# A two-layer hybrid transformer on one core: w_out, w_o and the merge gates multiplied in 1024-column panels

## The chip, the core and the metric

The kernel runs on one NeuronCore of a Trainium2 chip, in fp32 throughout. The metric is the device time of one execution in microseconds (us), as a median over runs; lower is better. Engines are named as in the profile: PE is the matrix engine (TensorE) and PEld its weight loads, DVE is VectorE, ACT is ScalarE, POOL is GpSimd, SP only issues transfers here. The program is written with a tile framework: tiles come from pools with a fixed number of buffers, and a scheduler fixes, before the program ever runs, the order in which each engine's instructions stand. On the chip each engine takes its own list in that order and waits at an instruction until what it needs is there.

## The reference

256 tokens of width 2048 pass through two layers and a last norm. Cut to what matters here:

```python
# layer 1
h = rmsnorm(x, g_mix) @ w_in                      # split into z, xBC, dt, q, k, v, qi, ki, wi
y_ssd = ssd(...) * silu(z), normed                # [256, 1024]
y_att = attention over the top keys               # [256, 1024]
x = x + concat(y_ssd, y_att) @ w_out              # w_out [2048, 2048]
x = x + square(relu(rmsnorm(x, g_mlp) @ w_up)) @ w_down
# layer 2
h = rms_norm(x, ln1_w) @ w_in_2                   # 10792 columns; the last 4096 are two merge gates
o_a = nsa_attention(...)                          # compressed, selected and window branch, [256, 1024]
o_b = gated_delta_rule(...)                       # [256, 1024]
m = sigmoid(gate_a) * (o_a @ w_pa) + sigmoid(gate_b) * (o_b @ w_pb)
x = x + m @ w_o                                   # w_o [2048, 2048]
x = x + square(relu(rms_norm(x, ln2_w) @ w_up_2)) @ w_down_2
out = rms_norm(x, ln_f_w)
```

## The kernel before

**One product is three matmuls.** Every fp32 operand is split into a high part rounded to fp32r and a low part, the rest. A product of a 128 x 128 block of activations (the left side, held as `xh`, `xl`) with a 128 x 512 block of weights (`wa`, `wb`) is xh wa + xh wb + xl wa, three matmuls of 512 columns that add up in one PSUM bank. Weights stream in from HBM once, 1 MB at a time, into a ring of three tiles `wst`; ACT rounds each 128 x 1024 half into `whi`, DVE subtracts it into `wlo`. There are four buffers of `whi` and four of `wlo`.

**Two ways to multiply a matrix.** `panel` makes 512 columns: for each of 16 k-tiles and both token halves one product, so 96 matmuls, into two PSUM banks, one of the tag `mm0` and one of `mm1`. `wide` makes 1024 columns for 256 tokens and takes the k-tiles in eight pairs. Six pairs are plain (eight products each). Two pairs, `SPAIRS = (2, 5)`, are multiplied as 2 x 2 blocks by seven products in place of eight (the Winograd form of Strassen's method): the weight sums `t13` and `t24` are made by DVE, the sums of the left side come from `forms`, made once (`a_forms`). `wide` needs eight accumulators at once: P2, P3, P4 and E from its first product on, P1, P5, P6 and P7 from the first seven-product pair on. `shared` adds them up to the four outputs.

**PSUM has eight banks,** in four tags of two: `mm0`, `mm1`, `tp` (transposes) and `sx` (small products of the attentions and scans). `panel` uses the first two tags alone. `wide` uses all four; it takes P2, P3, P4 and E from `mm0` and `mm1` when a counter `turn` is even and from `tp` and `sx` when it is odd, the other four accumulators from the other two tags, and adds 1 to `turn`. A tile of a tag can only be written once the tile before the last one of this tag has been read for the last time.

**Where it is used before.** `wide` makes w_up and w_down of both layers (15 calls in each layer; the last of w_down is `panel` twice). `panel` makes everything else: w_in, w_out (in four panels, the k-tiles of the attention half first), the merge gates (L1298), w_pb and w_pa (L1301), w_o (L1327).

**The order around the places that change.** In layer 1 the tail of the SSD scan (lines L715 to L754, products in `sx`, then L772, L777 and the transposes of `xsd` in `tp` by `x_to_act`, L345) is written just ahead of w_out. In layer 2 the attention (from L1078 to L1290: transposes in `tp`, scores and outputs in `sx`) is written just ahead of the merge: first o_b with `gate_b` and w_pb, then o_a with `gate_a` and w_pa. A group of the attention is two heads: scores against two kinds of keys (L1256), softmax for two token halves and two kinds (L606 add, L611 max, L616 exp, L618 to L621, L622 scaling), transposes of the probabilities (L1266, L1271, copied out by L1268 and L1273; the compressed branch's L1279, copied by L1281), and the outputs (L1286 to L1290). There are four such groups. The transposes of O (L876) and the small products that make the compressed keys come ahead of them.

Of the kernel before, what the change touches and what calls it, by code (L numbers as in the profile page):

```python
# [57 lines left out]
def build(ctx, tc, I, out, tap=None, upto=99):  # L58
# [176 lines left out]
    def wide(w, r0, c0, lhs, forms):  # L235
# [8 lines left out]
        ns = len(SPAIRS)  # L244
# [20 lines left out]
        for j in range(8):  # L265
# [3 lines left out]
            if j not in SPAIRS:  # L269
# [96 lines left out]
    def flat(ap):  # L366
        return ap.rearrange("p k c -> p (k c)")

    def ffn(X, act, forms, w_up, w_down, r, after, tail=0):
        for s_ in range(4):  # L370
# [27 lines left out]
            for P in range(2):  # L398
# [8 lines left out]
                out_ = shared(B)  # L407
                for i, l, part, bank in out_:
                    x = X[2 * P + 1 - l][:, i]
                    V.tensor_tensor(x, part, x, op=OP.add)  # L410
                for i, l, part, bank in out_:
                    x = X[2 * P + 1 - l][:, i]
                    V.tensor_tensor(x, bank, x, op=OP.add)
# [401 lines left out]
    ffn(X, xn, xforms, I["w_up"][0], I["w_down"][0], r, after1)  # L815
# [478 lines left out]
    M = []  # L1294
    for which, (o_, w_, mc) in enumerate(((ob, "w_pb_2", 2048), (oa, "w_pa_2", 0))):
        for p in range(4):
            ps = panel(w_in2, 0, 16, 6696 + mc + p * 512, 512, at_k(xn))
# [28 lines left out]
    for p in range(4):  # L1326
        ps = panel(I["w_o_2"][0], 0, 16, p * 512, 512, at_k(M))  # L1327
        for t in range(2):
            V.scalar_tensor_tensor(X[p][:, t], ps[t], 0.5, X[p][:, t], op0=OP.mult, op1=OP.add)
        q = quarter("xn")  # L1330
        x_to_act(X[p], q, g_ln2[:, 4 * p:4 * p + 4], xforms, p)
        xn.append(q)
        for t in range(2):
            sumsq(ssx[:, t, p:p + 1], X[p][:, t])
# [52 lines left out]
```

## Time and profile before

| | |
|---|---|
| median of 3 runs | 2650.08 us (2646.22 to 2652.0) |
| the profiled execution, its own time | 2654.01 us |
| its span, first to last instruction | 2652.2 us |
| PE busy | 2623.1 us, 99% |
| DVE, ACT busy | 1917.3 us (72%), 1411.5 us (53%) |
| mean granted TensorE clock | 0.997 of full |

Busy is the time in which an engine has at least one instruction under way. A matmul is shown for longer than it holds the next one back, since matmuls are pipelined: a 512-column matmul is shown with some 0.39 us, and the next starts 0.23 us later. So the time of a stretch of PE is read from how many matmuls start in it.

### The profile page before, as it was taken

The numbers are of one execution on the slowest core, as the hardware profiler recorded it, in microseconds if no ns is written. First come the engines' busy times: TensorE is split into PE (matmuls) and PEld (weight loads), VectorE is DVE, ScalarE is ACT, GpSimd is POOL, SyncE is SP. The second block draws the span as 40 slices with busy tenths as digits, with TensorE's granted clock in tenths as the row PEclk, the third lists the DMA queues.
The fourth block names the chain that finished last, engine by engine and source line by source line (L and its number), as shares of the span: only waits on it lengthen the run. The fifth ranks groups of instructions, "written<-read, shape, count | busy, mean of one in ns | idle before, by whom it ended". The sixth has DMA issues, their size and how long they took to land.

```text
span 2652.2 us, 32498 instructions
## 1 busy us (share of the span) xinstructions
PE 2623.1 (99%) x12656; PEld 2195.1 (83%) x12656; DVE 1917.3 (72%) x2593; ACT 1411.5 (53%) x1876; POOL 39.2 (1%) x46
## 2 busy tenths in 40 slices
PE   8999999999999999999999999999999999999998
PEld 8998888888887888888888887888888888888887
DVE  5767767787887887676754767455678888888886
ACT  5465455546556556554533554444456455465564
POOL 0000000000000000000100000000000000000000
PEclk9999999999999999999999999999999999999999
DMA  7454555565555555653432743556555555555544
GB/s 237 144 172 159 175 188 182 175 207 191 190 205 176 191 191 191 213 194 127 131 97 86 252 161 113 181 191 212 193 190 176 207 200 183 203 190 191 206 175 175
DMA packets 192153, 478.63 MB, mean 180 GB/s; under 512 B 9128, under 2 KB 50047, under 8 KB 191999
## 3 DMA queue, kind: packets, MB, share of 16 engines
q1 hardware_dynamic: 185840, 467.57, 52.3%
q10 hardware_dynamic: 6158, 8.99, 1.0%
q8 instruction: 99, 1.62, 0.2%
q14 instruction: 56, 0.45, 0.0%
HBM read 472.32 MB, written 4.21 MB: 180 GB/s over the span
## 4 chain that ended last, share of the span: by engine, by line
PE 92%; DMA 3%; DVE 2%; ACT 2%; issue 1%; ACTq 0%; POOL 0%; POOLq 0%; SPq 0%; DVEq 0%
PE mm L250 21%; PE mm L193 13%; PE mm L194 13%; PE mm L192 13%; PE tp L250 11%; PE sx L250 10%; DMA wst<-in_w_down_dram 2%; DVE wlo L262 2%; PE sx L982 1%; ACT whi L261 1%; PE sx L977 1%; PE tp L345 1%; PE mm L390 1%; DMA wst<-in_w_up_dram 1%; PE tp L876 0%
## 5 line engine op out<-in xcount | busy, mean ns | idle before, releaser
L208 DVE TENSOR_TENSOR wlo<-wst,whi 128x1024 fp32r<-128x1024 f32 (+6 forms) x416 | 475.8, 1147 | 321.6 <-ACT whi L207 320.7
L261 ACT ACTIVATE whi<-wst 128x1024 fp32r<-128x1024 f32 x480 | 476.8, 1005 | 379.3 <-PE mm L250 164.1
L207 ACT ACTIVATE whi<-wst 128x1024 fp32r<-128x1024 f32 (+6 forms) x416 | 414.7, 998 | 467.4 <-PE mm L194 437.2
L262 DVE TENSOR_TENSOR wlo<-wst,whi 128x1024 fp32r<-128x1024 f32 x480 | 543.5, 1155 | 140.7 <-ACT whi L261 133.1
L193 PE MATMUL mm<-wlo,x2h 128*128 128x512 f32 (+3 forms) x736 | 279.4, 380 | 0.8 <-DVE wlo L208 0.8
L194 PE MATMUL mm<-whi,x2l 128*128 128x512 f32 (+3 forms) x736 | 279.3, 380 | 0.0
L192 PE MATMUL mm<-whi,x2h 128*128 128x512 f32 (+3 forms) x736 | 279.1, 380 | 0.0
L261 ACT ACTIVATE whi<-t 128x1024 fp32r<-128x1024 f32 x120 | 127.3, 1061 | 150.5 <-PE mm L250 76.8
L262 DVE TENSOR_TENSOR wlo<-t,whi 128x1024 fp32r<-128x1024 f32 x120 | 146.9, 1224 | 80.1 <-ACT whi L261 79.7
L250 PE MATMUL mm<-whi,xnh 128*128 128x512 f32 x432 | 169.0, 391 | 0.0
L250 PE MATMUL mm<-whi,xnl 128*128 128x512 f32 x432 | 168.4, 390 | 0.0
L250 PE MATMUL mm<-wlo,xnh 128*128 128x512 f32 x432 | 168.2, 389 | 0.0
L193 PEld LDWEIGHTS mm<-wlo,x2h 128*128 128x128 f32 x736 | 139.0, 189 | 21.2 <-DVE wlo L208 1.4
L192 PEld LDWEIGHTS mm<-whi,x2h 128*128 128x128 f32 x736 | 139.0, 189 | 20.2 <-issue 1.1
L194 PEld LDWEIGHTS mm<-whi,x2l 128*128 128x128 f32 x736 | 138.9, 189 | 19.9 <-issue 0.9
L192 PE MATMUL mm<-whi,xnh 128*128 128x512 f32 (+3 forms) x416 | 153.0, 369 | 2.0 <-ACT whi L207 1.6
L193 PE MATMUL mm<-wlo,xnh 128*128 128x512 f32 (+3 forms) x416 | 152.2, 366 | 0.0
L194 PE MATMUL mm<-whi,xnl 128*128 128x512 f32 (+3 forms) x416 | 150.9, 366 | 0.1
L250 PE MATMUL mm<-whi,hTh 128*128 128x512 f32 x378 | 148.4, 393 | 0.0
L250 PE MATMUL mm<-wlo,hTh 128*128 128x512 f32 x378 | 147.7, 391 | 0.0
L250 PE MATMUL mm<-whi,hTl 128*128 128x512 f32 x378 | 147.5, 390 | 0.0
L250 PEld LDWEIGHTS mm<-whi,xnl 128*128 128x128 f32 x432 | 81.1, 188 | 17.0
(532 smaller groups left out, 5303.7 us busy)
## 6 DMA issues: line engine op xcount, KB each, us to landing
wst<-in_w_up_dram SPq DMA_DIRECT2D x128, 1024.0 KB, 4.9
wst<-in_w_down_dram SPq DMA_DIRECT2D x128, 1024.0 KB, 5.5
wst<-in_w_in_dram SPq DMA_DIRECT2D x84, 1024.0 KB, 5.0
wst<-in_w_out_dram SPq DMA_DIRECT2D x16, 1024.0 KB, 5.2
wst<-in_w_o_dram SPq DMA_DIRECT2D x16, 1024.0 KB, 5.0
wst<-in_w_in_dram SPq DMA_DIRECT2D x16, 780.0 KB, 4.4
wst<-in_w_in_dram SPq DMA_DIRECT2D x12, 824.0 KB, 4.5
wst<-in_w_in_dram SPq DMA_DIRECT2D x12, 736.0 KB, 6.3
```

What stands on the lines that cost most here:

```text
L192: PE.matmul(ps[t][:, :n], xh[:, sl], wa, start=kt == first, stop=False)
L193: PE.matmul(ps[t][:, :n], xh[:, sl], wb, start=False, stop=False)
L194: PE.matmul(ps[t][:, :n], xl[:, sl], wa, start=False, stop=kt == last)
L207: S.activation(a[:, :2 * n], src, AF.Copy)
L208: V.tensor_tensor(b[:, :2 * n], src, a[:, :2 * n].bitcast(F32), op=OP.subtract)
L250: PE.matmul(B[b], x, y, start=left[b] == total[b], stop=left[b] == 1)
L261: S.activation(a[:, :n], src, AF.Copy)
L262: V.tensor_tensor(b[:, :n], src, a[:, :n].bitcast(F32), op=OP.subtract)
L345: PE.transpose(ps[:, kk, t, :], x[:, t, (k0 + kk) * 128:(k0 + kk + 1) * 128], ident)
L390: PE.transpose(pv[:, kk, t, :], us[t, l][:, c:c + 128], ident)
L977: PE.matmul(ps[:, i * 64:(i + 1) * 64].rearrange("p (m b) -> p m b", b=b), N[:, i], half(T[:, i], 0), start=True, stop=True)
L982: PE.matmul(ps[:, i * 64:(i + 1) * 64].rearrange("p (m b) -> p m b", b=b), P[:, i], half(Tt[:, i], 1), start=True, stop=True)
```

## The change

w_out and w_o become two calls of `wide` each, and each merge gate becomes two. The sums of the left side, which the feed-forward layers make on the way from the transposes, are made here by a new helper `forms_of` from the two parts (high plus low) of the activations that are there already. `wide` takes the number of its seven-product pairs from `forms` and the order of the pairs as an argument: w_out uses the pairs 5 and 7 in the order 4, 5, 6, 7, 0, 1, 2, 3. The code that adds the four outputs to X moves out of `ffn` into `add_blocks`; `add_wide` replaces `add_panel`. The factor 0.5 of w_o moves into the split of M. Calls of `wide` now stand ahead of the two feed-forward layers, so that `turn` is 0 and 1 at w_out, 17 to 20 at the merge gates, 21 and 22 at w_o.

```diff
+    def forms_of(act, pairs):
+
+        forms = {}
+        for j in pairs:
+            f = s2([128, 2, 2, 128], name="ff")
+            k0 = 2 * (j % 2)
+            h, l = (flat(a[:, k0:k0 + 2]).bitcast(F32) for a in act[j // 2])
+            V.tensor_tensor(f.rearrange("p k t c -> p (k t c)"), h, l, op=OP.add)
+            a_forms(f, forms, j)
+        return forms
+
-    def wide(w, r0, c0, lhs, forms):
+    def wide(w, r0, c0, lhs, forms, order=range(8)):
...
-        ns = len(SPAIRS)
+        ns = len(forms)
...
-        for j in range(8):
+        for j in order:
...
-            if j not in SPAIRS:
+            if j not in forms:
...
+    def add_blocks(B, P):
+        out_ = shared(B)
+        for i, l, part, bank in out_:
+            x = X[2 * P + 1 - l][:, i]
+            V.tensor_tensor(x, part, x, op=OP.add)
+        for i, l, part, bank in out_:
+            x = X[2 * P + 1 - l][:, i]
+            V.tensor_tensor(x, bank, x, op=OP.add)
...
-    def add_panel(ps, p, scale, act, gain, ssx, forms):
-        for t in range(2):
-            V.scalar_tensor_tensor(X[p][:, t], ps[t], scale, X[p][:, t], op0=OP.mult, op1=OP.add)
-        q = quarter("xn")
-        x_to_act(X[p], q, gain[:, 4 * p:4 * p + 4], forms, p)
-        act.append(q)
-        for t in range(2):
-            sumsq(ssx[:, t, p:p + 1], X[p][:, t])
+    def add_wide(w, act, P, xn, gain, ssx, forms, xforms, order=range(8)):
+        B, _ = wide(w, 0, P * 1024, at_k(act), forms, order)
+        add_blocks(B, P)
+        for p in (2 * P, 2 * P + 1):
+            q = quarter("xn")
+            x_to_act(X[p], q, gain[:, 4 * p:4 * p + 4], xforms, p)
+            xn.append(q)
+            for t in range(2):
+                sumsq(ssx[:, t, p:p + 1], X[p][:, t])
...
-    for p in range(4):
-        ps = panel(I["w_out"][0], 0, 16, p * 512, 512, at_k(mix), order=list(range(8, 16)) + list(range(8)))
-        add_panel(ps, p, 1.0, xn, g_mlp, ssx, xforms)
+    forms = forms_of(mix, (5, 7))
+    for P in range(2):
+        add_wide(I["w_out"][0], mix, P, xn, g_mlp, ssx, forms, xforms, (4, 5, 6, 7, 0, 1, 2, 3))
...
     M = []
+    forms = forms_of(xn, SPAIRS)
     for which, (o_, w_, mc) in enumerate(((ob, "w_pb_2", 2048), (oa, "w_pa_2", 0))):
-        for p in range(4):
-            ps = panel(w_in2, 0, 16, 6696 + mc + p * 512, 512, at_k(xn))
-            th = sp([128, 2, 512], name="mth")
-            for t in range(2):
-                S.activation(th[:, t], ps[t], AF.Tanh, scale=rh[:, t:t + 1])
-            ps = panel(I[w_][0], 0, 8, p * 512, 512, at_k(o_))
...
+        for P in range(2):
+            B, _ = wide(w_in2, 0, 6696 + mc + P * 1024, at_k(xn), forms)
+            ths = {}
+            for i, l, part, bank in shared(B):
+                V.tensor_tensor(part, bank, part, op=OP.add)
+                S.activation(part, part, AF.Tanh, scale=rh[:, i:i + 1])
+                ths[2 * P + 1 - l, i] = part
+            for p in (2 * P, 2 * P + 1):
+                ps = panel(I[w_][0], 0, 8, p * 512, 512, at_k(o_))
...
-    for p in range(4):
-        ps = panel(I["w_o_2"][0], 0, 16, p * 512, 512, at_k(M))
-        for t in range(2):
-            V.scalar_tensor_tensor(X[p][:, t], ps[t], 0.5, X[p][:, t], op0=OP.mult, op1=OP.add)
...
+    forms = forms_of(M, SPAIRS)
+    for P in range(2):
+        add_wide(I["w_o_2"][0], M, P, xn, g_ln2, ssx, forms, xforms)
```

The scheduler sets the order anew. Three places of PE's list follow; L1256 and the like are lines of before, and the attention's lines have moved down by 15 in the changed kernel (L1256 is L1271 now); L192 to L194 are the three matmuls of `panel`, L261 (L250 before) those of `wide`.

**PE in the second group of the attention, before.** The scores of a group (into `sx`), and what stands between them and behind them: w_pb's panel (`mm_`; obh and obl are the parts of o_b).

```order
L1256 MATMUL sx<-ksT,nqT 128x128 x2
L192 MATMUL mm_13585<-whi,obh 128x512
L193 MATMUL mm_13585<-wlo,obh 128x512
L194 MATMUL mm_13585<-whi,obl 128x512
L1256 MATMUL sx<-ksT,nqT 128x256 x2
L1256 MATMUL sx<-kwT,nqT 128x128 x2
L192 MATMUL mm_13586<-whi,obh 128x512
L193 MATMUL mm_13586<-wlo,obh 128x512
L1256 MATMUL sx<-kwT,nqT 128x256 x2
L194 MATMUL mm_13586<-whi,obl 128x512
L192 MATMUL mm_13585<-whi,obh 128x512
L193 MATMUL mm_13585<-wlo,obh 128x512
```

The same place in the changed kernel, from the scores to the transposes of both kinds of keys:

```order
L1271 MATMUL sx<-ksT,nqT 128x128 x2
L1271 MATMUL sx<-ksT,nqT 128x256 x2
L1271 MATMUL sx<-kwT,nqT 128x128 x2
L1271 MATMUL sx<-kwT,nqT 128x256 x2
L1281 MATMUL tp<-idt,NP_13235 128x128
L1281 MATMUL tp<-idt,NP_13250 128x128
L1281 MATMUL tp<-idt,NP_13235 128x128
L1281 MATMUL tp<-idt,NP_13250 128x128
L1286 MATMUL tp<-idt,NP_13250 128x128 x2
L1281 MATMUL tp<-idt,NP_13277 128x128
L1281 MATMUL tp<-idt,NP_13292 128x128
L1281 MATMUL tp<-idt,NP_13277 128x128
```

The panel's matmuls that stood between the scores and the transposes are gone from there. No matmul of a panel or of `wide` stands between the first transposes of O and the last four transposes of the fourth group, which follow here, with what comes behind them (`x2h` is the left side of the merge gate):

```order
L1294 MATMUL tp<-idt,Pc_13076 15x128
L1294 MATMUL tp<-idt,Pc_13102 15x128
L1294 MATMUL tp<-idt,Pc_13076 15x128
L1294 MATMUL tp<-idt,Pc_13102 15x128
L261 MATMUL tp<-whi,x2h 128x512
L261 MATMUL tp<-wlo,x2h 128x512
L261 MATMUL tp<-whi,x2l 128x512
L261 MATMUL tp<-whi,x2h 128x512
L1301 MATMUL sx<-NTc,vcm 128x2x128
```

So the merge gate begins behind the last transposes of the attention, with accumulators in `tp` and `sx`; before, 298 matmuls of panels stood in that stretch.

**PE at the end of the SSD scan, before.** The scan's last product (L751) stands fourteen matmuls ahead of the first transposes of `xsd` (L345), which are for the first half of y_ssd; between and behind them stands w_out's first panel on the attention half (`yatt`):

```order
L192 MATMUL mm_2979<-whi,yatth 128x512
L193 MATMUL mm_2979<-wlo,yatth 128x512
L194 MATMUL mm_2979<-whi,yattl 128x512
L192 MATMUL mm_2980<-whi,yatth 128x512
L345 MATMUL tp<-idt,xsd 128x128 x2
L193 MATMUL mm_2980<-wlo,yatth 128x512
L345 MATMUL tp<-idt,xsd 128x128 x6
L194 MATMUL mm_2980<-whi,yattl 128x512
L192 MATMUL mm_2979<-whi,yatth 128x512
```

The same place in the changed kernel (L765 is the scan's last product, L356 the transposes for both halves; `sfh` is a left sum of `forms`):

```order
L761 MATMUL sx<-xdd,Bm 128x512
L754 MATMUL sx<-xdt,E 128x64 x4
L261 MATMUL mm_3004<-whi,yattl 128x512
L765 MATMUL sx<-ST,acc 128x512
L356 MATMUL tp<-idt,xsd 128x128 x16
L261 MATMUL mm_3002<-whi,sfh 128x512
L261 MATMUL mm_3002<-wlo,sfh 128x512
L261 MATMUL sx<-whi,sfh 128x512
```

The first pair of `wide`, 24 matmuls of which the last is shown, lies ahead of the scan's last product. Between that and the sixteen transposes there is no matmul now, and the pair behind them (`sfh`) puts products into `tp`, which the transposes use first.

## Rows read from the trace of the kernel before

**Rows 1.** The page's head: span, then busy time, share and instructions of each engine.

```profile
span 2652.2 us, 32498 instructions
PE 2623.1 (99%) x12656; PEld 2195.1 (83%) x12656; DVE 1917.3 (72%) x2593; ACT 1411.5 (53%) x1876; POOL 39.2 (1%) x46
```

**Rows 2.** Stretches: start:end, length, busy time and instructions by engine, granted clock, DMA.

```profile
core 0: us, PE busy (x) PEld busy (x) DVE busy (x) ACT busy (x) POOL busy (x), PEclk, DMA share, GB/s
1662.00:1860.00 198.00, 198.00 (x888) 163.84 (x886) 101.61 (x97) 86.51 (x90) 0.00 (x0) 1.00 0.59 197
2048.00:2122.00 74.00, 74.00 (x328) 61.33 (x327) 62.39 (x70) 37.52 (x39) 0.00 (x0) 1.00 0.57 201
1560.60:1564.10 3.50, 3.50 (x32) 3.43 (x31) 0.00 (x0) 1.38 (x3) 0.00 (x0) 1.00 0.51 196
1564.10:1570.90 6.80, 6.80 (x23) 5.86 (x23) 2.88 (x20) 1.72 (x5) 0.00 (x0) 0.50 0.00 0
```

**Rows 3.** Stretches for line L193 alone, one panel matmul in three.

```profile
321.50:334.10 12.60, 5.88 (x15) 2.63 (x14) 1.00 0.61 191
1540.30:1569.10 28.80, 8.70 (x21) 4.10 (x21) 0.91 0.42 141
1540.30:1656.10 115.80, 40.47 (x100) 19.00 (x99) 0.97 0.35 117
```

**Rows 4.** Timeline: first transposes of O; first scores of each group on DVE.

```profile
1540.39 1.03 PE L876 MATMUL tp<-idt,O 128*128 128x128 f32 x8
...
1569.15 0.42 DVE L606 TENSOR_TENSOR NP<-sx,Bt 128x256 f32<-128x256 f32 x1 [1.86 <-PE sx L1256]
...
1592.66 0.43 DVE L606 TENSOR_TENSOR NP<-sx,Bt 128x256 f32<-128x256 f32 x1 [2.30 <-PE sx L1256]
...
1615.35 0.42 DVE L606 TENSOR_TENSOR NP<-sx,Bt 128x256 f32<-128x256 f32 x1 [4.93 <-PE sx L1256]
...
1638.66 0.42 DVE L606 TENSOR_TENSOR NP<-sx,Bt 128x256 f32<-128x256 f32 x1 [5.39 <-PE sx L1256]
```

**Rows 5.** Timeline of DVE's softmax: second kind of keys (group 1), first kind's end (2).

```profile
1577.53 0.43 DVE L1273 COPY NT<-tp 128x256 f32<-128x256 f32 x1
...
1579.78 1.22 DVE L208 TENSOR_TENSOR wlo<-wst,whi 128x1024 fp32r<-128x1024 f32 x1
...
1582.99 0.69 DVE L622 TENSOR_TENSOR NP<-NP,su 128x512 f32<-128x512 f32 x1
...
1597.69 0.69 DVE L622 TENSOR_TENSOR NP<-NP,su 128x512 f32<-128x512 f32 x1
...
1599.31 0.42 DVE L1273 COPY NT<-tp 128x256 f32<-128x256 f32 x1 [0.59 <-PE tp L1271]
```

**Rows 6.** Timeline of a group's tail: probabilities out, outputs, next scores.

```profile
1654.95 0.52 PE L1266 MATMUL tp<-idt,NP 128*128 128x128 f32 x3
...
1656.16 0.61 PE L1279 MATMUL tp<-idt,Pc 128*15 128x128 f32 x4
...
1657.63 0.69 PE L1286 MATMUL sx<-NTc,vcm 15*128 15x256 f32 x2
...
1661.34 0.60 PE L1290 MATMUL sx<-NT,KVw 128*128 128x256 f32 x2
...
1638.02 0.61 PE L1256 MATMUL sx<-ksT,nqT 128*128 128x128 f32 x4
```

**Rows 7.** Timeline from the SSD scan's last product to y_ssd's last low parts.

```profile
321.55 1.02 PE L751 MATMUL sx<-ST,acc 128*128 128x512 f32 x2
...
323.28 1.22 DVE L208 TENSOR_TENSOR wlo<-wst,whi 128x1024 fp32r<-128x1024 f32 x1
...
328.71 1.60 POOL L159 TENSOR_TENSOR rg<-rv,mhalf 128x2 f32<-128x2 f32 x1 [3.66 <-DVE rv L157]
...
333.61 1.90 DVE L174 SCALAR_TENSOR_TENSOR yssdl<-tp,P1T,yssdh 128x256 fp32r<-128x256 f32 x4
```

**Rows 8.** Groups by line and shape: count, busy us, mean ns, idle us before and releaser.

```profile
L390 PE MATMUL mm<-idt,cu 128*128 128x128 f32 x64 | 15.6, 285 | 4.5 <-ACT cu L378 4.5
L390 PE MATMUL tp<-idt,cu 128*128 128x128 f32 x32 | 8.9, 291 | 5.3 <-ACT cu L378 5.3
```

More of the change, by code (lines that the diff above doesn't have):

```diff
@@ L367, in flat, with ffn @@
         return ap.rearrange("p k c -> p (k c)")
-    def ffn(X, act, forms, w_up, w_down, r, after, tail=0):
+    def add_blocks(B, P):
[6 more added lines that the diff above has]
+            V.tensor_tensor(x, bank, x, op=OP.add)
+    def ffn(act, forms, w_up, w_down, r, after, tail=0):
         for s_ in range(4):
@@ L406, in ffn @@
                 B, _ = wide(w_down, s_ * 2048, P * 1024, at_k(hT), hforms)
[L407 to L413, printed above, removed]
+                add_blocks(B, P)
                 if s_ == 3:
@@ L783, in build @@
     ssx = tiny([128, 2, 4], "ssx", bufs=2)
[L785 to L792 removed]
+    def add_wide(w, act, P, xn, gain, ssx, forms, xforms, order=range(8)):
+        B, _ = wide(w, 0, P * 1024, at_k(act), forms, order)
+        add_blocks(B, P)
+        for p in (2 * P, 2 * P + 1):
[4 more added lines that the diff above has]
+                sumsq(ssx[:, t, p:p + 1], X[p][:, t])
     X = x_panels()
@@ L813, in after1 @@
             nc.scalar.dma_start(xsave[:, p], X[p])
-    ffn(X, xn, xforms, I["w_up"][0], I["w_down"][0], r, after1)
+    ffn(xn, xforms, I["w_up"][0], I["w_down"][0], r, after1)
     if upto == 2:
@@ L1294, in build @@
     M = []
+    forms = forms_of(xn, SPAIRS)
     for which, (o_, w_, mc) in enumerate(((ob, "w_pb_2", 2048), (oa, "w_pa_2", 0))):
-        for p in range(4):
-            ps = panel(w_in2, 0, 16, 6696 + mc + p * 512, 512, at_k(xn))
-            th = sp([128, 2, 512], name="mth")
-            for t in range(2):
-                S.activation(th[:, t], ps[t], AF.Tanh, scale=rh[:, t:t + 1])
-            ps = panel(I[w_][0], 0, 8, p * 512, 512, at_k(o_))
-            if which == 0:
-                m = sp([128, 2, 512], name="M")
-                M.append(m)
-                for t in range(2):
-                    V.scalar_tensor_tensor(m[:, t], th[:, t], 1.0, ps[t], op0=OP.add, op1=OP.mult)
-            else:
-                for t in range(2):
-                    V.scalar_tensor_tensor(th[:, t], th[:, t], 1.0, ps[t], op0=OP.add, op1=OP.mult)
-                    V.tensor_tensor(M[p][:, t], M[p][:, t], th[:, t], op=OP.add)
+        for P in range(2):
[7 more added lines that the diff above has]
+                ps = panel(I[w_][0], 0, 8, p * 512, 512, at_k(o_))
+                if which == 0:
+                    m = sp([128, 2, 512], name="M")
+                    M.append(m)
+                    for t in range(2):
+                        V.scalar_tensor_tensor(m[:, t], ths[p, t], 1.0, ps[t], op0=OP.add, op1=OP.mult)
+                    continue
+                for t in range(2):
+                    th = ths[p, t]
+                    V.scalar_tensor_tensor(th, th, 1.0, ps[t], op0=OP.add, op1=OP.mult)
+                    V.tensor_tensor(M[p][:, t], M[p][:, t], th, op=OP.add)
                 q = quarter("mT")
@@ L1317, in build @@
                             PE.transpose(pv[:, kk, t], M[p][:, t, (k0 + kk) * 128:(k0 + kk + 1) * 128], ident)
-                    split(pt, flat(q[0][:, k0:k0 + 2]), flat(q[1][:, k0:k0 + 2]))
+                    split(pt, flat(q[0][:, k0:k0 + 2]), flat(q[1][:, k0:k0 + 2]), 0.5)
                 M[p] = q
@@ L1325, in build @@
     ssx = tiny([128, 2, 4], "ssx", bufs=2)
-    for p in range(4):
-        ps = panel(I["w_o_2"][0], 0, 16, p * 512, 512, at_k(M))
-        for t in range(2):
-            V.scalar_tensor_tensor(X[p][:, t], ps[t], 0.5, X[p][:, t], op0=OP.mult, op1=OP.add)
[L1330 to L1334, printed above, removed]
+    forms = forms_of(M, SPAIRS)
+    for P in range(2):
+        add_wide(I["w_o_2"][0], M, P, xn, g_ln2, ssx, forms, xforms)
     r = x_rstd(ssx, "r4")
@@ L1361, in after2 @@
         nc.sync.dma_start(o[:, 1024:1536], X[2][:, t])
-    ffn(X, xn, xforms, I["w_up_2"][0], I["w_down_2"][0], r, after2, tail=8)
+    ffn(xn, xforms, I["w_up_2"][0], I["w_down_2"][0], r, after2, tail=8)
 _INS = ["x", "g_mix", "w_in", "conv_w", "conv_b", "dt_bias", "a_log", "d_skip", "g_ssd", "g_q", "g_k", "g_kidx",
```

## The prediction, made before the changed kernel had run

> **What bounds the kernel now.** I read the page's head first: PE is busy for 2623.1 of 2652.2 us [rows 1], so time goes where PE starts matmuls, and any hole in its list is lost. Then the stretches. In 74 us of `wide` in a feed-forward layer 328 matmuls start, one in 0.2256 us; DVE is busy for 62.4 of these 74 us, 84%, so it keeps up there [rows 2]. In the panels of the merge it is busy for 101.6 of 198 us, 51% [rows 2]. Both ways of multiplying are bound by the number of matmuls. The third view is what PE does while DVE and ACT work through a chain of small steps: in the 115.8 us of the attention one panel line of three has 100 matmuls, two of which began before it, and at the end of the SSD scan one has 15 in 12.6 us [rows 3]. Panels fill PE while it would wait for softmax. The change touches just these panels.
>
> **What the change removes.** A 2048 x 2048 matrix costs four panels of 96 matmuls, 384; two calls of `wide` cost 2 x (6 x 24 + 2 x 21) = 372. Four such matrices (w_out, two gates, w_o) give 48 matmuls fewer, 48 x 0.2256 = **10.8 us** less.
>
> **What it moves, the attention.** `panel` used `mm0` and `mm1` alone, so it could run while the attention held `tp` and `sx`. `wide` needs all four tags, and `turn` is 17 at the first gate, so its first four accumulators are the ones in `tp` and `sx`: it can't start while the attention passes tiles through these. The order shows what the scheduler made of that: no matmul of a weight matrix from the first transposes of O to the last transposes of the fourth group, 298 before; w_pb stands behind the gate and comes no earlier. The 298 are not lost, they run later. What is lost is the cover: PE's time in that stretch is now as long as the chain, T, and before its own work and small waits in it took 115.8 - 298 x 0.2256 = 48.6 us. The loss is T - 48.6.
>
> T by pieces. The head, from the first transposes of O to the first scores on DVE, took 1569.15 - 1540.39 = 28.8 us [rows 4]; 61 panel matmuls (3 x 21 less the two that began before) were in it [rows 3], 13.8 us. If they all delayed it, it takes 15.0 us bare, if none, 28.8; I take the middle, 21.9, since handovers between small instructions make most of it but ACT and DVE also split weights there. A group took 23.5, 22.7 and 23.3 us [rows 4]. Bare, by steps: softmax for the first kind of keys 1592.66 to 1598.38, 5.7 us, in which DVE split no weights [rows 4, 5]; to the copy of the transposes 0.9 [rows 5]; from such a copy to the end of the second softmax 1577.53 to 1583.68, 6.2 us with one split of 1.22 in it [rows 5], of which I keep 5.4; then the tail, which the fourth group shows: its last transposes begin at 1654.95, some 0.15 us after the scaling, and its outputs end at 1661.94 [rows 6], 7.1; scores until DVE has them, 1638.02 to 1638.66, 0.6 [rows 4, 6]. Sum 19.8 us. All of that with PE at full clock. PE hardly works during the softmaxes, and what the clock does then one stretch tells: after 3.5 us in which PE issued only tiny products (32, of 7 to 15 columns for the most part) the granted clock was 0.50 for 6.8 us, that is 1.2 GHz in place of 2.4 [rows 2]. At that level the outputs, 4.3 us from 1657.63 to 1661.94 [rows 6], take some 3.4 more (what is not waiting doubles), and some twenty scores and transposes on the path, 0.11 us each [rows 4, 6], another 2.1. I take the outputs at half and the rest at full clock, 23.2, near 23: **what the panels took away from DVE, the clock takes back**. So T = 21.9 + 3 x 23 + 14.0 (the fourth group without outputs and scores: 5.7 + 0.9 + 5.4 + 2.0) = 104.9, and the loss is **56.3 us**. Bounds: 15.0 + 3 x 19.8 + 14.0 = 88.4, a loss of 39.8; and 28.8 + 3 x 25.3 + 15.3 = 120, a loss of 71.4.
>
> On the clock the Trainium skill (TensorE: Matmul & The Clock Gate, section "What's actually happening") says that the throttled state is the default and activity releases it; the 0.50 of [rows 2] agrees. By that rule all of the bare stretch would run at 1.2 GHz, which is rival 2 below; by the full clock of the rows around it, the group's 19.8 us would stand.
>
> The first matmuls of the gate then start at half clock: 6.8 us at half [rows 2] cost **3.4 us**, bounds 0 and 6.8 (if w_out pays the same).
>
> **What it moves, the SSD scan.** In w_out only pair 4 fits beside the scan (`mm` tags); pair 5 needs `tp`, which y_ssd's transposes use. From the scan's last product to the last low part of y_ssd is 321.5 to 335.5 us [rows 7]; in the 12.6 us to 334.1 stood some 42 panel matmuls (3 x 15, less those at the edges) [rows 3], 9.5 us of cover. The chain behind it, DVE, POOL's power of 1.60 us twice [rows 7], transposes, split, stays; DVE loses about two splits of 1.22 us and gets sums for `forms` in their place, perhaps 1.2 us less. After the transposes 16 products can run before the split of `t24` is there, about 1.9 us short. 9.5 - 1.2 + 1.9, **10 us**, bounds 6 and 13 (half clock behind the hole).
>
> **What it adds.** `forms_of`, `t13` and `t24` for eight calls, additions in `shared`: on DVE, hidden where `wide` runs as in the feed-forward layers, at 84% [rows 2], and at the first gate behind 48 matmuls (10.8 us) of two plain pairs whose weights are split early. Without that cover it would be some 5 us for each matrix (two times add, four small sums, split). At the border between two calls the transposes wait for the last addition, with four to nine matmuls to fill. Such borders in w_up wait 9.8 us in 16 calls [rows 8], 0.6 each; four borders at w_out and w_o, **2.5 us**, bounds 0 and 8 (each near 2). The DMAs stay as many and as large on SP's queue, of 2 k-tiles x 1024 columns in place of 4 x 512; w_up's have that shape already, in the stretch at 0.2256 us [rows 2].
>
> **Sum.** -10.8 + 56.3 + 3.4 + 10 + 2.5 = +61.4. On the profiled execution, 2654.0, that is 2715; the median of the runs shown is 3.9 us lower, so I forecast **2712 us** for the median. With all low ends 2650.1 - 10.8 + 39.8 + 6 = 2685, with all high ends 2650.1 - 10.8 + 71.4 + 6.8 + 13 + 8 = 2739.
>
> **Rivals.**
> 1. The chain hurries: with no weights to split, DVE and ACT answer at once and the clock recovers in every burst. For it: the head's bare bound, and the first softmax without a split, 5.7 us. Against it: the 0.50 row, and 19.8 us for a group is already the sum without splits. T = 88.4, 2652.5 + 39.8 - 56.3 = about 2695 us.
> 2. All of the stretch at half clock: T = 120, 2712 + 15 = 2727 us. For it the 0.50 row; against it that the clock was full again after 6.8 us.
> 3. DVE becomes the bound in w_out and at the gate, where sums of the left side come on top of 84%: 5 us for each of three matrices more, 2727 us. Against it the slack at the panels of w_pb and w_pa between.
> 4. The other side: PE is not held up, because it starts the gate's matmuls past the attention's waiting ones. Then the 48 matmuls count and the rest stays hidden: 2650.1 - 10.8 + 2.5 = 2642 us, faster. It decides from the point where T falls to 48.6 us, or where PE leaves the order of its list. Against it: four groups of two softmaxes are 44 us on DVE and ACT [rows 5], and outputs, scores and head stand in series with them.
> The Trainium skill (TensorE: Matmul & The Clock Gate, "Step-by-step: what each phase is for") says that matmuls stay in program order and only weight loads are pulled ahead, which speaks against rival 4; in the rows shown PE's starts follow its list.
>
> **How the numbers follow.** The forecast as summed 0.56, rival 1 0.17, rival 2 0.14, rival 3 0.09, rival 4 0.04. The range 2688 to 2738 takes in rivals 1 to 3 but for their outer tails, which with rival 4 are 2 in 10. About 0.2%, 5.3 us, is what a measurement of this kernel can tell from no change. Only rival 4 is faster (0.03) or the same (0.01), all others slower, 0.96.
>
> **What would show it.** In the changed profile: about 105 us from the first transposes of O to the fourth group's last, with PE busy for less than half of it and a granted clock near 0.5 in much of it; groups 23 us apart on DVE though it splits no weights; a hole of 8 to 10 us after the scan's last product; elsewhere 0.2256 us a matmul and 48 matmuls fewer. I am wrong if the groups come 17 us apart or less, if matmuls of the gate start among the attention's, or if holes appear inside the `wide` calls that follow.

## The result, and the profile after

The changed kernel takes **2723.77 us** (median of 5 runs, 2719.12 to 2727.02) against 2650.08 (2646.22 to 2652.0): ratio 1.0278, 95% interval 1.0263 to 1.0294. It is 73.7 us slower; forecast were 2712, in a range of 2688 to 2738. Its profiled execution took 2723.77 us as well, 69.8 more than the one of before (2654.01), and the accounts below are made against those 69.8.

The page's head of the changed kernel answers to [rows 1]: PE is busy 19 us longer with 48 matmuls fewer, and the span holds 69.7 us more, so 51 us of it are PE standing still.

```profile
span 2721.9 us, 32676 instructions
...
PE 2642.0 (97%) x12608; PEld 2201.6 (81%) x12608; DVE 2034.0 (75%) x2773; ACT 1446.8 (53%) x1922; POOL 38.9 (1%) x46
```

The windows of the changed kernel (columns as in [rows 2]): first the five pieces of the attention, from the first transposes of O over the first scores of each group on DVE (they answer to [rows 4]) to the first matmul of the gate; then the start of the gate; then w_out behind the scan's last product; last a stretch of `wide` in a feed-forward layer.

```profile
1549.20:1576.20 27.00, 18.19 (x98) 13.92 (x96) 11.04 (x30) 10.29 (x21) 0.00 (x0) 0.67 0.19 71
1576.20:1600.50 24.30, 16.58 (x48) 10.81 (x48) 11.32 (x45) 5.80 (x20) 0.00 (x0) 0.59 0.00 0
1600.50:1624.30 23.80, 15.36 (x48) 9.86 (x48) 10.77 (x32) 5.61 (x20) 0.00 (x0) 0.64 0.00 0
1624.30:1648.20 23.90, 15.37 (x48) 9.86 (x48) 10.85 (x33) 5.71 (x20) 0.00 (x0) 0.64 0.00 1
1648.20:1662.50 14.30, 6.64 (x28) 4.53 (x29) 10.11 (x31) 5.20 (x19) 0.00 (x0) 0.71 0.00 1
...
1549.20:1662.50 113.30, 72.13 (x269) 48.99 (x268) 54.08 (x168) 32.62 (x97) 0.00 (x0) 0.65 0.05 17
1662.50:1666.40 3.90, 3.90 (x13) 2.37 (x12) 2.70 (x7) 0.63 (x1) 0.00 (x0) 0.76 0.00 0
...
320.40:323.50 3.10, 0.63 (x2) 0.00 (x0) 2.65 (x7) 0.84 (x1) 1.07 (x1) 0.91 0.00 0
323.50:333.20 9.70, 6.40 (x22) 4.78 (x23) 8.70 (x21) 5.84 (x13) 1.07 (x1) 0.50 0.00 0
...
2117.00:2191.00 74.00, 74.00 (x328) 61.28 (x327) 62.38 (x70) 37.72 (x39) 0.00 (x0) 1.00 0.58 204
```

Five things are to be read here. The attention, with 269 instructions of PE where it had 298 matmuls of panels besides, lasts 113.3 us. Its groups are 23.8 to 24.3 us apart, no closer than before (22.7 to 23.5), though DVE is busy for 11 us of a group. The granted clock is 0.59 to 0.71, that is at the lower level (0.50) for most of the time. Transfers stop (0 GB/s): the three weight tiles are emptied by ACT and DVE, whose buffers of split weights are full, and no matmul takes from these; the last split of weights on DVE ahead of the gate starts at 1553.21 us. And in the feed-forward layer nothing has changed, 328 matmuls in 74 us to the matmul.

What PE waited for in that stretch (the waits of PE; line, releaser: sum, times, longest): each wait is for a step of softmax or of the small chains. The first row names ACT's exponential; the scaling on DVE (L636), which follows it, is the last step before these transposes.

```profile
PE tp L1281 <- ACT NP L630: 17.7, 7, 3.6
PE tp L1281 <- DVE NP L636: 8.8, 9, 1.5
PE tp L1152 <- DVE gy L1149: 6.9, 2, 4.2
PE sx L1271 <- DVE NP L620: 2.6, 6, 0.5
```

And the timeline at two places: the end of the scan (answers to [rows 7]), and the head of the attention on PE and DVE.

```profile
320.01 1.02 PE L765 MATMUL sx<-ST,acc 128*128 128x512 f32 x2
323.56 1.97 PE L356 MATMUL tp<-idt,xsd 128*128 128x128 f32 x8 [2.53 <-DVE xsd L791]
328.77 1.94 PE L356 MATMUL tp<-idt,xsd 128*128 128x128 f32 x8 [3.24 <-DVE xsd L791]
330.37 0.78 PE L261 MATMUL mm<-whi,sfh 128*128 128x512 f32 x1
...
333.46 0.48 DVE L174 SCALAR_TENSOR_TENSOR yssdl<-tp,P1T,yssdh 128x256 fp32r<-128x256 f32 x1 [0.41 <-ACT yssdh L170]
...
1549.27 1.03 PE L891 MATMUL tp<-idt,O 128*128 128x128 f32 x8
...
1552.36 1.31 PE L891 MATMUL tp<-idt,O 128*128 128x128 f32 x8 [1.51 <-DVE obl L174]
...
1549.69 1.23 DVE L290 TENSOR_TENSOR t<-wst 128x1024 f32<-128x1024 f32 x1 [0.63 <-DMA wst<-in_w_in_dram]
1550.95 0.69 DVE L293 TENSOR_TENSOR t<-wst,t 128x512 f32<-128x512 f32 x1
1551.56 1.40 DVE L174 SCALAR_TENSOR_TENSOR obl<-tp,P1T,obh 128x512 fp32r<-128x512 f32 x2
```

Behind the scan PE stands twice, 2.53 and 3.24 us, and all that it does from 323.5 to 333.2 runs at a clock of 0.50. In the head DVE makes `t13` and half of `t24` for the gate (L290, L293) ahead of the low part of o_b that the next transposes wait for.

**The account** of the profiled execution. For the waits I take of each gap between two starts on PE what is above the median gap of matmuls of that shape (half clock counts as a wait too), and sum over a stretch. w_out and the first call of w_up: 18.6 us against 5.5 before, +13.1, of which +10.3 between the scan's last product and 358 us and the rest at the borders. The attention: 113.3 - 48.6 = +64.7. From the gate's first matmul to the end of w_o: 5.8 against 2.7, +3.1. The 48 matmuls: -10.8. Sum +70.1, measured 69.8.

### The profile page after: what moved, and what is told of

It reads as the page before. It is cut to its first block, busy times and chain, and to the rows that moved or that the text cites. A ratio compares the mean times of both kernels' runs of the same rounds, so it can differ in the third digit from the quotient of the medians.

```text
span 2721.9 us, 32676 instructions
## 1 busy us (share of the span) xinstructions
PE 2642.0 (97%) x12608; PEld 2201.6 (81%) x12608; DVE 2034.0 (75%) x2773; ACT 1446.8 (53%) x1922; POOL 38.9 (1%) x46
## 4 chain that ended last, share of the span: by engine, by line
PE 86%; DVE 5%; DMA 4%; ACT 3%; issue 1%; ACTq 0%; POOL 0%; POOLq 0%; SPq 0%; DVEq 0%
PE mm L261 25%; PE tp L261 13%; PE sx L261 12%; PE mm L194 8%; PE mm L193 8%; PE mm L192 8%; DVE wlo L273 2%; DMA wst<-in_w_down_dram 2%; ACT whi L272 1%; PE sx L997 1%; PE sx L992 1%; PE tp L356 1%; PE mm L410 1%; ACT NP L630 1%; PE sx L1303 1%
## 5 line engine op out<-in xcount | busy, mean ns | idle before, releaser
L272 ACT ACTIVATE whi<-wst 128x1024 fp32r<-128x1024 f32 x608 | 603.4, 1005 | 484.5 <-PE mm L261 197.2
L273 DVE TENSOR_TENSOR wlo<-wst,whi 128x1024 fp32r<-128x1024 f32 x608 | 688.3, 1154 | 181.7 <-ACT whi L272 172.7
L208 DVE TENSOR_TENSOR wlo<-wst,whi 128x1024 fp32r<-128x1024 f32 (+6 forms) x288 | 319.0, 1111 | 182.5 <-ACT whi L207 181.8
L207 ACT ACTIVATE whi<-wst 128x1024 fp32r<-128x1024 f32 (+6 forms) x288 | 279.2, 971 | 302.4 <-PE mm L194 253.1
L193 PE MATMUL mm<-wlo,x2h 128*128 128x512 f32 (+3 forms) x480 | 178.0, 371 | 1.4 <-DVE wlo L208 1.4
L192 PE MATMUL mm<-whi,x2h 128*128 128x512 f32 (+3 forms) x480 | 177.3, 370 | 0.0
L194 PE MATMUL mm<-whi,x2l 128*128 128x512 f32 (+3 forms) x480 | 177.3, 369 | 0.0
L261 PE MATMUL mm<-whi,xnh 128*128 128x512 f32 x432 | 168.9, 391 | 0.0
L261 PE MATMUL mm<-whi,xnl 128*128 128x512 f32 x432 | 168.4, 390 | 0.0
L261 PE MATMUL mm<-wlo,xnh 128*128 128x512 f32 x432 | 168.2, 389 | 0.0
L192 PE MATMUL mm<-whi,xnh 128*128 128x512 f32 (+3 forms) x416 | 152.4, 368 | 2.0 <-ACT whi L207 1.6
L193 PE MATMUL mm<-wlo,xnh 128*128 128x512 f32 (+3 forms) x416 | 151.6, 365 | 0.0
L194 PE MATMUL mm<-whi,xnl 128*128 128x512 f32 (+3 forms) x416 | 150.4, 364 | 0.1
L261 PE MATMUL mm<-whi,hTh 128*128 128x512 f32 x378 | 148.3, 392 | 0.0
L261 PE MATMUL mm<-whi,hTl 128*128 128x512 f32 x378 | 147.6, 391 | 0.0
L261 PE MATMUL mm<-wlo,hTh 128*128 128x512 f32 x378 | 147.6, 390 | 0.0
L290 DVE TENSOR_TENSOR t<-wst 128x1024 f32<-128x1024 f32 x76 | 92.7, 1220 | 29.5 <-DMA wst<-in_w_down_dram 19.1
L193 PEld LDWEIGHTS mm<-wlo,x2h 128*128 128x128 f32 x480 | 90.5, 188 | 12.4 <-DVE wlo L208 2.0
L194 PEld LDWEIGHTS mm<-whi,x2l 128*128 128x128 f32 x480 | 90.4, 188 | 10.4 <-issue 0.9
L192 PEld LDWEIGHTS mm<-whi,x2h 128*128 128x128 f32 x480 | 90.4, 188 | 10.0 <-issue 0.6
```

The source lines that it names most:

```text
L192: PE.matmul(ps[t][:, :n], xh[:, sl], wa, start=kt == first, stop=False)
L193: PE.matmul(ps[t][:, :n], xh[:, sl], wb, start=False, stop=False)
L194: PE.matmul(ps[t][:, :n], xl[:, sl], wa, start=False, stop=kt == last)
L207: S.activation(a[:, :2 * n], src, AF.Copy)
L208: V.tensor_tensor(b[:, :2 * n], src, a[:, :2 * n].bitcast(F32), op=OP.subtract)
L261: PE.matmul(B[b], x, y, start=left[b] == total[b], stop=left[b] == 1)
```

## Experiments

The theory was **lost cover**: no matmul got slower, but PE has nothing to do while the attention and the scan hold `tp` and `sx`, since the call that comes next wants these banks. The rivals: the wide calls themselves cost time (sums on DVE, borders, half clock), and, for the size of the loss, that the groups are set by handovers and the clock is only an outcome. The first four kernels ran side by side on one chip (before: 2649.78), the others in three more groups; each ratio is formed over all runs of a kernel, against the kernel before on the same chip (2649.78 to 2651.75), and can differ a little from that of the medians.

**1. The first gate in narrow panels again.**

```diff
+        if which == 0:
+            for p in range(4):
+                ps = panel(w_in2, 0, 16, 6696 + mc + p * 512, 512, at_k(xn))
...
+            continue
```

> The changed kernel with the first merge gate (gate_b) in narrow panels again; w_out, gate_a and w_o stay in 1024-column panels. Theory 'lost cover': the attention gets its 298 matmuls of panels back, so what stays is w_out's net loss, +8.9 us (the first transposes of O came at 1549.3 in the changed kernel and at 1540.4 before), and 24 matmuls fewer behind it, -5.4, with 0 to 2 us of borders: 2653 to 2656 us. Rival 'the wide calls themselves': wide is slower than panels at these matrices, by DVE's sums, the borders or the half clock at its start; then half or more of the loss that is left stays, over 2670 us.

Measured 2659.35 us, ratio 1.0037 (1.0023 to 1.0051). 64 of the 74 us are gone with this one matrix. The 3 us above the expectation are w_out's: I had taken its loss from one shift of 8.9 us between two executions, and in that shift lies the scatter of the feed-forward layer (its waits in layer 1, with the same code, are 9.9 to 14.1 us in the profiled executions of this study).

**2. w_out narrow as well.** Its four panels as before, so that only gate_a and w_o are wide.

> As the run before, and w_out in narrow panels too, so that only gate_a and w_o are multiplied in 1024-column panels (24 matmuls fewer than before). Theory 'lost cover': neither place has an attention or a scan in front of it, so the fewer matmuls count: 2650.1 - 24 x 0.2256 + 0 to 2 us of borders = 2645 to 2647 us. Rival 'the wide calls themselves': 2650 us or more.

Measured 2646.42 us, ratio 0.9988 (0.9979 to 0.9997), and once more, side by side with the kernels of experiment 9:

> The kernel with only gate_a and w_o in 1024-column panels once more, beside the two others on one chip: 2645 to 2648 us, as measured in its first run (2646.4); what the two others have less or more than this is what gate_b's second half and w_out bring.

There 2648.05, at the edge of what was expected, with 2651.75 before, 0.9988 (0.9980 to 0.9997). Where nothing stands ahead that needs `tp` and `sx` for itself, wide gives back 3.4 to 3.7 of the 5.4 us. The difference to run 1, 12.9 us, is what w_out costs: with the 2.7 us that it saves, 15.6 us of loss, and 13.1 by the account above.

**3. The kernel before, with two banks exchanged.** The sharpest test, since it adds no work at all.

```diff
-    def panel(w, r0, KT, c0, n, lhs, order=None, before=None, tail=0):
-        ps = [psum(f"mm{t}", [128, 512]) for t in range(2)]
+    def panel(w, r0, KT, c0, n, lhs, order=None, before=None, tail=0, tags=("mm0", "mm1")):
+        ps = [psum(k, [128, 512]) for k in tags]
...
+            ps = panel(..., tags=("tp", "sx") if which == p == 0 else ("mm0", "mm1"))
```

> The kernel before, all panels narrow, but the very first panel of the merge takes its two accumulators from tp and sx in place of mm0 and mm1. Not one matmul more or less, no sums, no wide call. Theory 'lost cover': the panel can't start while the attention passes tiles through tp and sx, and all panels behind it wait with it, so the attention lies bare as in the changed kernel: 2650.1 + 64 (112.7 us bare less 48.6 of its own work) + 3 of half clock = 2715 to 2718 us. Rival 'the wide calls themselves': 2650 to 2655 us.

Measured 2716.69 us, ratio 1.0256 (1.0242 to 1.0270): 66.9 us for the two banks of one panel. Its windows, the four groups and then the head:

```profile
1561.50:1585.90 24.40, 17.38 (x49) 11.45 (x48) 11.31 (x44) 5.97 (x21) 0.00 (x0) 0.57 0.00 0
1585.90:1609.90 24.00, 15.47 (x49) 9.95 (x48) 10.81 (x32) 5.67 (x19) 0.00 (x0) 0.64 0.00 1
1609.90:1633.80 23.90, 15.43 (x48) 9.97 (x48) 10.82 (x32) 5.67 (x19) 0.00 (x0) 0.64 0.00 0
1633.80:1648.00 14.20, 6.48 (x30) 4.51 (x30) 10.13 (x31) 5.07 (x18) 0.00 (x0) 0.74 0.00 0
1536.30:1561.50 25.20, 17.64 (x97) 13.43 (x95) 8.72 (x26) 10.01 (x21) 0.00 (x0) 0.68 0.21 77
```

The groups are those of the changed kernel to 0.2 us, at the same clock. The head is 1.8 us shorter (25.2 for 27.0), and what DVE doesn't have in it are the weight sums shown above (L290 and L293, 1.9 us) and the other half of `t24`, 0.7 us. PE's waits for the two steps behind these sums are 1.2 us shorter (0.7 and 3.9 for 1.5 and 4.2 us); the rest, some 0.7 us, is not shown to be theirs, since the clock falls at another point of the head in the two runs. So the banks explain the attention's loss; the wide call adds 1 to 2 us to it.

**4. w_out's sums last.** On run 1, w_out with `forms_of(mix, (2, 3))` in place of `(5, 7)`, in the same order: four plain pairs stand beside the scan's tail.

> As the first of these runs (gate_b narrow), and w_out takes its seven-product pairs from the half of y_ssd, pairs 2 and 3, which stand last, so that the four pairs of the attention half are plain and need only mm0 and mm1 while the scan's tail uses tp and sx. Theory 'lost cover' for w_out too: its loss of 11.6 us (8.9 net and 2.7 of matmuls saved) goes, 2650.1 - 36 x 0.2256 + 0 to 3 us of borders = 2642 to 2645 us. Rival: w_out loses by the sums of its left side and by its borders, which are the same here: 2653 to 2656 us as in the first run.

Measured 2658.26 us, ratio 1.0031 (1.0020 to 1.0042): missed. The hole at the scan is gone (waits from 320.4 to 358 us 0.8 where the changed kernel has 11.3), but at the two borders behind w_out's calls they are 7 and 2 us longer than in the kernel before. The timeline of PE at the first border:

```profile
363.10 0.50 PE L261 MATMUL sx<-whi,yatth 128*128 128x512 f32 x1 [0.82 <-DVE cu L320]
...
366.10 0.44 PE L356 MATMUL tp<-idt,X 128*128 128x128 f32 x2 [1.12 <-DVE X L387]
367.30 0.88 PE L356 MATMUL tp<-idt,X 128*128 128x128 f32 x6 [0.76 <-DVE X L387]
368.43 0.80 PE L261 MATMUL sx<-wlo,yatth 128*128 128x512 f32 x1 [0.26 <-DVE wlo L273]
369.02 0.63 PE L261 MATMUL sx<-whi,yattl 128*128 128x512 f32 x1
```

With both seven-product pairs at the end, DVE comes late to the border, makes the eight additions of `shared` and X there, and PE waits for them; then it works at half clock (0.63 in place of 0.39 us). These waits would make some 2654 us; the other 4 are open. The waits are read from one execution each, and such readings scatter by about that much (9.9 to 14.1 us, run 1).

**5. PE filled with dead matmuls.**

```diff
+                fl = psum("mm0", [128, 512])
+                for i in range(24):
+                    PE.matmul(fl, xn[0][0][:, 0, :128], flat(xn[0][0][:, 0:2]), start=i == 0, stop=i == 23)
                 ps = psum("tp", [128, 512])
```

> The changed kernel with 192 more matmuls of 512 columns (43 us of PE at 0.2256 us) that multiply a part of the left side by itself into a bank of mm0 that nobody reads; they have no weights to split, and the scheduler puts 47 in the head of the attention, some 44 in each of the groups 1 to 3 and 14 in the last. They give PE work there and nothing to DVE or ACT. Theory 'the clock takes back what DVE gains' (the prediction's): with PE filled the granted clock stays at 1.00 and a group of the attention falls from 24 us towards the 19.8 summed at full clock, 20 to 21.5 with the fillers in the way: the kernel gets faster by 8 to 14 us though it multiplies more, 2710 to 2716 us. Rival 'handovers between DVE and ACT set the groups, the clock is only an outcome': groups stay at 24 us, 2724 to 2730 us.

Measured 2712.07 us, ratio 1.0229 (1.0215 to 1.0243): 11.7 us faster than the changed kernel with 192 matmuls more. Its windows, the four groups and then the head:

```profile
1573.60:1593.30 19.70, 19.70 (x95) 15.16 (x94) 11.30 (x44) 5.70 (x20) 0.00 (x0) 0.98 0.00 1
1593.30:1612.60 19.30, 19.29 (x93) 14.18 (x92) 10.73 (x32) 5.75 (x20) 0.00 (x0) 1.00 0.00 1
1612.60:1631.90 19.30, 19.29 (x93) 14.18 (x92) 10.73 (x32) 5.75 (x20) 0.00 (x0) 1.00 0.00 0
1631.90:1646.00 14.10, 9.07 (x44) 6.35 (x43) 10.05 (x31) 5.33 (x19) 0.00 (x0) 0.88 0.01 2
1548.80:1573.60 24.80, 24.78 (x145) 19.79 (x144) 11.00 (x29) 10.03 (x21) 0.00 (x0) 0.95 0.21 76
...
1645.70:1700.00 54.30, 54.30 (x217) 42.92 (x215) 35.73 (x45) 24.63 (x28) 0.00 (x0) 0.90 0.39 135
```

DVE and ACT do the same work as in the changed kernel to 0.2 us a group, only the clock differs, 1.00 for 0.64, and a group takes 19.3 us in place of 24. At full clock the chain needs that at most: PE is busy throughout in the groups 1 to 3, so the filling itself may hold it up. The attention is 16.1 us shorter (97.2); some 4.5 come back behind it, where the last group, with few fillers, leaves the gate's first stretch at a clock of 0.90 over 54.3 us (the changed kernel has 0.76 over 3.9 us there). The rival, clock as a mere outcome, falls.

**6. Plain pairs first.**

```diff
+    turn[0] += 1
     forms = forms_of(xn, SPAIRS)
...
+            B, _ = wide(..., forms, (0, 1, 3, 4, 6, 7, 2, 5) if which == P == 0 else range(8))
```

> The changed kernel with turn raised by 1 ahead of the merge, so that the first gate call takes its first four accumulators from mm0 and mm1, and with its pairs in the order 0, 1, 3, 4, 6, 7, 2, 5: six plain pairs, 144 matmuls, need no bank of the attention. The order of PE puts these 144 into the head and the first group of the attention. Theory 'lost cover': they fill 144 x 0.2256 = 32.5 us of waiting, and the clock in the head and the first group stays up (0 to 5 us more): 2723.8 - 32.5 = 2686 to 2692 us. Rival 'any wide call stalls there', by DVE's sums or the transfers: no less than 2715 us.

Measured 2699.85 us, ratio 1.0185 (1.0171 to 1.0199), some 24 us back where 32 to 38 were expected. Its head and first group, which hold the 144 matmuls, and the second:

```profile
1545.40:1574.80 29.40, 29.38 (x158) 23.55 (x157) 13.35 (x30) 14.37 (x25) 0.00 (x0) 0.90 0.39 137
1574.80:1603.40 28.60, 28.60 (x133) 22.61 (x133) 23.30 (x58) 13.13 (x29) 0.00 (x0) 0.98 0.29 95
1603.40:1627.60 24.20, 15.99 (x54) 10.15 (x53) 11.65 (x33) 6.55 (x21) 0.00 (x0) 0.65 0.05 19
```

The clock is back at 0.98 as expected, and the group is still 4.3 us longer than the bare one. DVE is busy for 23.3 us of it, 12 more than in the changed kernel, since weights want splitting again, but it isn't what sets the length: PE is busy for all of the 28.6 us. Some 84 matmuls of the gate start in the group (some 48 of the x133 are the attention's own), 84 x 0.2256 = 19.0 us, and leave 9.6 us for the attention's own work. The same group in the kernel before, with some 60 panel matmuls (13.5 us), takes 23.5 us and leaves 10.0:

```profile
1569.15:1592.66 23.51, 23.51 (x109) 18.29 (x109) 17.62 (x50) 12.29 (x29) 0.00 (x0) 0.96 0.32 99
```

The head is as before too (29.4 us here and 28.8 there [rows 4], with some 61 matmuls in each). So in both pieces the cover is whole again, and what failed in the expectation is that all 144 would stand in waiting time: some 24 of them stand where none was left, while the groups behind stay bare (24.2 us at a clock of 0.65).

**7. w_out's sums in the middle.** As run 4, with `(0, 1)`: behind the plain pairs of the attention half, ahead of two plain pairs.

> As the first of the runs (gate_b narrow, the three others in 1024-column panels), but w_out's seven-product pairs are the pairs 0 and 1: behind the four plain pairs of the attention half, which cover the scan's tail, and ahead of the plain pairs 2 and 3, which cover what DVE owes before the border to the next call. In the run with the sums in the pairs 2 and 3 the hole at the scan was gone and the waits had moved to the two borders (7 and 2 us more than before there). Theory 'each of w_out's losses is a missing cover': both go, 2649.8 - 36 x 0.2256 + 2 to 5 us of what borders cost as in the other calls = 2643 to 2647 us. Rival 'DVE is the bound in w_out': the sums cost their time at any place, 2656 to 2660 us as in the two runs before.

Measured 2648.75 us, ratio 0.9992 (0.9983 to 1.0001). Some 11 us of w_out's losses are gone against run 1 by the place of its sums alone, which is against DVE as a bound at any place; but the 36 matmuls fewer give 2.1 us, not 3 to 7, and its interval still includes no gain. Three rows of its windows show what is left (PE 10.97 busy of 13, DVE 12.38): DVE works without a pause there, from the sums of y_ssd's left side through the weight sums and splits of both seven-product pairs, and PE waits for it.

```profile
320.00:345.00 25.00, 25.00 (x121) 20.26 (x120) 23.83 (x43) 13.88 (x23) 3.20 (x2) 1.00 0.43 137
345.00:358.00 13.00, 10.97 (x44) 7.75 (x43) 12.38 (x14) 7.20 (x9) 0.00 (x0) 1.00 0.58 181
358.00:385.00 27.00, 26.74 (x124) 21.23 (x123) 23.54 (x35) 16.97 (x28) 0.00 (x0) 1.00 0.56 188
```

**8. As much in wide panels as a cover is left for.** gate_b's first half stays narrow, its second half is wide; once with w_out wide (sums in the pairs 1 and 2), once with w_out narrow.

> All four matrices in 1024-column panels wherever a cover is left for what stands ahead: gate_b's first half stays in two narrow panels, interleaved with two of w_pb as before (288 matmuls of panels stand in the attention), its second half, gate_a and w_o are wide, and w_out is wide with its seven-product pairs 1 and 2, so that a plain pair of y_ssd (24 matmuls, 5.4 us) lies ahead of the first sums and one behind the last. 42 matmuls fewer than before. Theory 'each loss is a missing cover': 2650 - 42 x 0.2256 + 3 to 5 us for the borders and what is left at w_out (2.7 in the run with the pairs 0 and 1) = 2643.5 to 2645.5 us, a few us under the run with gate_a and w_o alone or level with it. Rival 'wide costs what it saves at these places': 2648 us or more.

> The same with w_out in narrow panels: gate_b's second half, gate_a and w_o wide, 30 matmuls fewer than before. Theory 'each loss is a missing cover': 2650 - 30 x 0.2256 + 1 to 3 us of borders = 2644 to 2646 us, and what this run has more than the one beside it is what w_out brings. Rival: 2648 us or more.

Measured 2649.73 us, ratio 0.9997 (0.9988 to 1.0006), and 2652.45, 1.0002 (0.9993 to 1.0011): both missed. The windows of the second, at the end of the attention:

```profile
1648.20:1651.10 2.90, 0.37 (x2) 0.00 (x0) 2.90 (x7) 1.06 (x1) 0.00 (x0) 1.00 0.50 203
1651.10:1654.10 3.00, 2.55 (x11) 1.89 (x12) 2.41 (x5) 0.60 (x1) 0.00 (x0) 0.54 0.25 37
```

288 matmuls of cover where 298 had stood end 2.9 us too early, and the attention's last transposes run at half clock (0.54). The wide half of gate_b has an odd `turn` and begins in `tp` and `sx`: the same fault, in small.

**9. The same two with `turn[0] += 1` ahead of the merge.**

> As the run with gate_b's second half, gate_a and w_o wide (w_out narrow), with turn raised by 1 ahead of the merge, so that the wide half of gate_b takes its first four accumulators from mm0 and mm1. In the run without that, the 288 matmuls of the panels ended at 1648.2 us, PE then stood 2.9 us and worked at half clock before the attention's last transposes at 1651; the order of PE now has 305 matmuls in the attention, 17 of them of the wide half. Theory 'lost cover': the 4 us come back and 30 x 0.2256 = 6.8 us less 1 to 3 us of borders stay: 2650 - 4 to 6 = 2644 to 2646 us. Rival 'six matmuls fewer at gate_b bring nothing, whatever covers the attention': level with or above that run, 2650 us or more.

> As the run with w_out's sums in its pairs 1 and 2, gate_b's second half, gate_a and w_o wide, with turn raised by 1 ahead of the merge in the same way. 42 matmuls fewer than before. Theory 'lost cover': 4 us under that run (2649.7), 2644 to 2647 us. Rival: 2649 us or more.

Measured 2645.23 us, ratio 0.9977 (0.9968 to 0.9986), and **2644.48**, ratio 0.9975 (0.9965 to 0.9985), each 5 to 7 us less than without that line. In the profiled execution of the first, PE no longer stands at the attention's end, nor does the clock fall there; its row answers to those of experiment 8:

```profile
1640.00:1654.60 14.60, 14.60 (x73) 11.76 (x73) 13.49 (x29) 8.62 (x17) 0.00 (x0) 1.00 0.43 144
```

The second has 42 of the 48 matmuls taken away and is faster than both kernels. How much of it w_out brings can't be told: 2644.48 and 2645.23 don't differ by more than their intervals. gate_b's second half brings 2.8 us beside the kernel with gate_a and w_o alone (2648.05 on the same chip), but the two intervals just overlap.

## Why the prediction was right

The direction, the place and the mechanism were right: 93% of the loss (75.0 of 80.9 us, before the matmuls saved) lies where the cover was lost at the attention (64.7 forecast 56.3) and at the scan (10.3, forecast 10), and for the attention run 3 shows that it is the banks. At w_out runs 4 and 7 show that it is the place of the seven-product pairs, which moves the banks and DVE's sums together. DVE's sums did not make the scan's chain longer than the splits did before (13.9 us from the last product to the last low part of y_ssd, 14.0 before [rows 7]), which speaks for the banks; but no run takes the two apart there. Of the 12 us by which the median missed its forecast, 8 are the chain below and 4 the step from the profiled execution to the median: the kernel before was profiled 3.9 us above its median, the changed one at it. Step by step:

- **Matmuls**, -10.8: as said; 328 in 74 us in the changed kernel too.
- **The attention's chain**, T = 104.9: measured 113.3. Mis-sized were the **head**, 27.0 for 21.9 (I took the middle between "all panel matmuls delayed it" and "none"; none was nearer: run 3, without the weight sums, has 25.2, and with its clock at 0.68 part of that is half clock, which my middle had only as far as the head before has it (0.91, [rows 3]); the weight sums add 1 to 2 us), and the **groups**, 24.0 for 23 three times. The last group was right, 14.3 for 14.0. The loss came out at 64.7, inside the bounds of 39.8 and 71.4.
- **"What the panels took away from DVE, the clock takes back"**: shown by run 5. The sum of 19.8 us at full clock is close to the measured 19.3 to 19.7, and half clock costs some 4.6 of the 24 us; I had 3.4. The row that I took for the clock was read too simply: of the 32 products ahead of the fall 24 have 7 or 15 columns, but six are transposes of 128 and two are panel matmuls of 512 columns, so PE did not issue "only tiny products".
- **The hole of w_out**, 10: measured 10.3, made of two waits of 2.5 and 3.2 us, and for the most part of the rest of half clock from 323.5 to 333.2. My sum had no half clock in it (only the upper bound of 13 had), and it had the chain shorter by 1.2 us, where it is as long as before (13.9 for 14.0); the number is right in part by luck.
- **Half clock at the gate, and borders**, 3.4 + 2.5: measured 3.1 for gate and w_o, and 2.8 at w_out's borders, 5.9 as forecast. The parts are not as forecast: 3.9 us at a clock of 0.76 cost about 1 us at the gate's start, so borders took nearly 5. That the sum agrees is luck.
- **Rivals.** Rival 1 (T = 88.4) is out: the groups come 24 us apart. (Its sum has a slip: with 2711.5 in place of 2652.5 it gives the 2695 us that stand there.) Rival 2 (T = 120, all at half clock) was nearer than I had it: the clock is 0.65 over the stretch, and T lies in the middle between my sum and it. By the rule of the Trainium skill (TensorE: Matmul & The Clock Gate, "What's actually happening") that the throttled state is the default and activity releases it, the low clock was to be the normal case there, and the rows bear that out for 70% of the time (a mean of 0.65 is 0.50 for 70% and 1.00 for 30%). Rival 3, DVE as the bound, holds at single places only (runs 4 and 7), not in the calls that follow. Rival 4 is out: no matmul of the gate starts ahead of the attention's last transposes.
- **One sign that I named was wrong**: PE was to be busy for less than half of the stretch. It is busy for 72.1 of 113.3 us, because at half clock what it does is shown for longer (0.63 in place of 0.39 us for a matmul of 512 columns, run 4).

## What to carry to other kernels

A way of multiplying with fewer matmuls that takes more banks of PSUM is paid at the place where its predecessor still works: ask for every such call which banks its first products want and who holds them then, and put the products that need only free banks first, spread over the whole stretch that wants cover (in run 6 they stood in its first half alone). Order its list so that the work that loads DVE (sums, splits) lies neither right behind such a chain nor right ahead of a border. The Trainium skill (Perfetto Trace Analysis, "Matmul Optimizations") tells to make use of all eight PSUM banks; run 3, which only moves one panel into banks that others need, is 66.9 us slower, so in this kernel the rule holds only where the banks are free at that time. Its other rule there, that matmuls should come back to back since the engine scales its power with its use, run 5 bears out (a clock of 1.00 for 0.64).

## What the runs showed of the hardware

In this kernel a chain of small steps over DVE, ACT and PE got faster when PE was given useless work beside it: with some 43 matmuls of 512 columns in each group the granted clock went from 0.64 to 1.00 and the group from 24.0 to 19.3 us, and 192 dead matmuls, 43 us of PE, made the kernel 11.7 us faster.
